# The lo half of stationary weights, 128 bytes further in SBUF

## The chip, the cores and the metric

The kernel runs on one core of a Trainium2 chip. The metric is the device time of one execution in microseconds (us), the median of several runs. Engines are called as in the profile: PE (TensorE matmuls), PEld (TensorE loading the stationary operand), DVE (VectorE), ACT (ScalarE), POOL (GpSimd), SP (the queue that issues DMAs).

## The reference, cut to what matters

Two layers of an encoder on 256 tokens of width 1024 in float32. Layer 0 is FFN, dilated attention, FFN; layer 1 is FFN, retention, FFN. Every sub-layer is normed before and after and added to the residual.

```
def swiglu(h, w_gate, w_up, w_down):
    return (jax.nn.silu(h @ w_gate) * (h @ w_up)) @ w_down
...
for i in range(DEPTH):                      # DEPTH = 2
    h = swiglu(rms_norm(x, g[0]), ...);  x = x + 0.5 * rms_norm(h, g[1])
    m = dilated_attention(...) if i % 2 == 0 else retention(...)
    x = x + rms_norm(m, g[3])
    h = swiglu(rms_norm(x, g[4]), ...);  x = x + 0.5 * rms_norm(h, g[5])
```

The widths: 1024 to 2816 for gate and for up, 2816 to 1024 for down (four such FFNs), 1024 to 9216 into attention, 1024 to 8192 into retention. Nearly all of the time goes to these products of 256 rows of input with a weight matrix that is read once from HBM.

## The kernel before, in words

**Three products for one.** Each float32 operand is cut into hi (rounded to the type float32r, which TensorE takes in one pass) and lo (what is left, also float32r). A product is then hi·hi + hi·lo + lo·hi, three matmuls into the same PSUM accumulator.

**The stream of weights.** `Stream` brings 128-row pieces of all weight matrices in the order in which they are used. A DMA of 1 MB on SP fills `raw` (two buffers); `split` then takes 1024 columns of it: ACT writes hi, scaled by the gain of the norm (line 121), DVE writes lo (line 122), in two halves of 512 columns. Both lie in one buffer `w` of a ring of six, each of 2112 floats per partition (`WC`, 64 floats more than the 2048 needed). A few pieces at the start of a sub-layer go to other buffers (`wx`, from `extra`), hi and lo at their start and middle. When PE has finished with a piece, `done` asks for the next split into that ring buffer.

**Two forms of matmul.** In `piece` and `down` (lines 192 to 194, helper `mm3`) 128 columns of the input are stationary, and 512 columns of the weight move. In `unit_t` (lines 381 to 383) it is the other way round: 128 columns of the weight are loaded as the stationary operand, and 256 columns of the input move. For each block of 128 weight columns there are three matmuls, which this document calls a triple:

```
mm(out, hi[:, s], xh, ...)   # line 381: load hi, move xh
mm(out, hi[:, s], xl, ...)   # line 382: load hi again, move xl
mm(out, lo[:, s], xh, ...)   # line 383: load lo, move xh
```

`unit_t` is used for all but the first gate and up block of each FFN, and for the queries and keys of the attention after its first unit. The pieces that it uses are marked in `Stream.still`.

**Where the operands lie.** Counted in bytes of one partition, modulo 256: the input tiles `xh` and `xl` lie at 0, with a row of 1280 bytes for each 128 channels, so that every moving operand begins at 0. The six ring buffers begin at 0 as well. In a piece that is in `still`, hi begins at 16 floats (64 bytes), and lo 1024 floats further, so at 64 again. The blocks of 128 columns are 512 bytes apart, so all loads of hi and of lo in `unit_t` begin at 64. In all other pieces hi and lo begin at 0.

The order of the work is the order in which the program is written; each engine takes its instructions in turn, and waits for others by semaphores.

Of the kernel before, what the change touches and what calls it, by code (L numbers as in the profile page):

```python
# [27 lines left out]
class Stream:  # L28
# [67 lines left out]
    def split(self):  # L96
        if self.n_split >= len(self.pieces):
            return
        i = self.n_split
        self.n_split += 1  # L100
        g, j, gain = self.pieces[i]
        while self.n_dma <= g:
            self.dma()
        nc = self.K.nc
        raw = self.raw[g][:, j * 1024 : (j + 1) * 1024]
        if i in self.extra:
            both = self.K.sb.tile([P, 2, 1024], F32R, tag=self.extra[i], name=f"wx{i}")
            hi, lo = both[:, 0], both[:, 1]
        else:

            both = self.K.sb.tile([P, WC], F32R, tag="w", bufs=self.ring, name=f"w{i}")
            o = 16 if i in self.still else 0
            hi, lo = (both[:, z : z + 1024] for z in (o, o + 1024))
        if gain is None:
            nc.scalar.activation(hi, raw, AF.Copy)  # L115
            nc.vector.tensor_tensor(out=lo, in0=raw, in1=hi.bitcast(F32), op=ALU.subtract)  # L116
        else:
            for kk in range(2):
                s = slice(kk * 512, kk * 512 + 512)
                gc = self.K.gcol[:, gain + kk : gain + kk + 1]  # L120
                nc.scalar.activation(hi[:, s], raw[:, s], AF.Copy, scale=gc)  # L121
                nc.vector.scalar_tensor_tensor(  # L122
                    out=lo[:, s], in0=raw[:, s], scalar=gc, in1=hi[:, s].bitcast(F32),
                    op0=ALU.mult, op1=ALU.subtract,
                )
        self.tiles[i] = (hi, lo)
        if j == 1:
            del self.raw[g]
            while self.n_dma < len(self.groups) and self.n_dma <= g + self.raw_bufs:
                self.dma()  # L130
# [927 lines left out]
```

## Time and profile before

| | |
|---|---|
| median of 3 runs (lowest to highest) | 1292.06 us (1289.16 to 1293.95) |
| the profiled execution, its own time | 1295.78 us |
| its span, first to last instruction | 1294.0 us |
| PE busy, PEld busy | 99%, 88% of the span |
| DVE, ACT, POOL busy | 69%, 54%, 2% |
| share of PE in the chain of work that ended last | 90% |
| granted TensorE clock | 0.998 |
| read from HBM | 232 MB, 180 GB/s over the span |

How to read it: matmuls are pipelined, each one's end is modelled, and the spans of matmuls that follow each other overlap. A busy PE is thus no measure of its pace. The pace is the distance from the start of a matmul to the start of the next, which the timeline gives. PEld overlaps with PE: while one matmul runs, the stationary operand of the next is loaded.

### The profile page before, as it was taken

How to read it: one execution, taken by the hardware profiler on the slowest of the kernel's cores; microseconds unless marked ns; L12 is line 12 of the kernel's file. 1: busy time of each engine (PE TensorE's matmuls, PEld its weight loads, DVE VectorE, ACT ScalarE, POOL GpSimd, SP SyncE). 2: the span in 40 equal slices, each digit the busy share in tenths (PEclk: the TensorE clock that was granted, in tenths of full speed). 3: DMA queues.
4: the chain of work that ended last, by engine and by line, in shares of the span. 5: the costliest groups of instructions: out<-in, count | busy, mean ns of one | idle time of the engine just before them, and what ended most of it. 6: DMA issues, size and time to landing. Idle time of an engine off the chain costs nothing.

```text
span 1294.0 us, 20715 instructions
## 1 busy us (share of the span) xinstructions
PE 1276.6 (99%) x8362; PEld 1136.7 (88%) x8362; DVE 889.4 (69%) x1593; ACT 695.5 (54%) x1073; POOL 19.7 (2%) x17
## 2 busy tenths in 40 slices
PE   8999999999999999999999999999999999999997
PEld 6999888987997879999889998877888888899986
DVE  6776557678567668866477665588887875767644
ACT  4655445467445557764456554455555545555442
POOL 1000001000000000000000000000000000000000
PEclk9999999999999999999999999999999999999999
DMA  7755566664764356665546565645564645565551
GB/s 217 229 186 193 189 217 192 200 200 146 201 198 153 130 162 221 196 196 179 192 163 209 187 195 194 197 147 175 155 184 144 186 165 195 168 200 176 190 195 65
DMA packets 130093, 235.72 MB, mean 182 GB/s; under 512 B 25404, under 2 KB 42284, under 8 KB 129997
## 3 DMA queue, kind: packets, MB, share of 16 engines
q1 hardware_dynamic: 129852, 234.14, 56.7%
q8 instruction: 65, 1.06, 0.3%
q14 instruction: 32, 0.25, 0.1%
q10 hardware_dynamic: 144, 0.26, 0.1%
HBM read 232.21 MB, written 1.12 MB: 180 GB/s over the span
## 4 chain that ended last, share of the span: by engine, by line
PE 90%; DVE 4%; ACT 2%; DMA 2%; issue 1%; SPq 0%; DVEq 0%; ACTq 0%
PE ac_f L381 10%; PE ac_f L382 10%; PE ac_f L383 10%; PE d_f L192 6%; PE d_f L193 6%; PE d_f L194 6%; PE rt L194 4%; PE rt L193 4%; PE rt L192 4%; PE at L382 3%; PE at L383 3%; PE at L381 3%; PE at L192 2%; PE at L194 2%; DMA raw<-in_ret_w_in_dram 2%; PE at L193 2%
## 5 line engine op out<-in xcount | busy, mean ns | idle before, releaser
L121 ACT ACTIVATE w<-raw,gcol 128x512 fp32r<-128x512 f32 x596 | 394.0, 715 | 309.0 <-PE ac_f L383 101.9
L122 DVE SCALAR_TENSOR_TENSOR w<-raw,gcol,w 128x512 fp32r<-128x512 f32 x596 | 418.1, 749 | 153.9 <-ACT w L121 150.6
L116 DVE TENSOR_TENSOR w<-raw,w 128x1024 fp32r<-128x1024 f32 x112 | 137.2, 1225 | 134.5 <-ACT w L115 134.2
L115 ACT ACTIVATE w<-raw 128x1024 fp32r<-128x1024 f32 x112 | 118.8, 1061 | 166.7 <-PE d_f L194 95.7
L192 PE MATMUL d_f<-w,hhf 128*128 128x512 f32 x352 | 137.2, 390 | 0.0
L193 PE MATMUL d_f<-w,hhf 128*128 128x512 f32 x352 | 137.0, 389 | 0.0
L194 PE MATMUL d_f<-w,hlf 128*128 128x512 f32 x352 | 137.0, 389 | 0.0
L382 PE MATMUL at<-xl_f,w 128*128 128x256 f32 x352 | 99.0, 281 | 0.0
L381 PE MATMUL at<-xh_f,w 128*128 128x256 f32 x352 | 99.0, 282 | 0.0
L383 PE MATMUL at<-xh_f,w 128*128 128x256 f32 x352 | 98.9, 281 | 0.0
L192 PE MATMUL rt<-w,xh_f 128*128 128x512 f32 x244 | 95.6, 392 | 0.2 <-ACT xh_f L238 0.2
L193 PE MATMUL rt<-w,xh_f 128*128 128x512 f32 x244 | 95.8, 392 | 0.0
L194 PE MATMUL rt<-w,xl_f 128*128 128x512 f32 x244 | 95.1, 390 | 0.0
L381 PE MATMUL ac_f<-xh_at,w 128*128 128x256 f32 x288 | 81.0, 281 | 0.0
L381 PE MATMUL ac_f<-xh_f,w 128*128 128x256 f32 x288 | 81.0, 281 | 0.0
L381 PE MATMUL ac_f<-xh_rt,w 128*128 128x256 f32 x288 | 81.0, 281 | 0.0
L383 PE MATMUL ac_f<-xh_f,w 128*128 128x256 f32 x288 | 80.9, 281 | 0.0
L383 PE MATMUL ac_f<-xh_rt,w 128*128 128x256 f32 x288 | 80.9, 281 | 0.0
L383 PE MATMUL ac_f<-xh_at,w 128*128 128x256 f32 x288 | 80.9, 281 | 0.0
L382 PE MATMUL ac_f<-xl_at,w 128*128 128x256 f32 x288 | 80.9, 281 | 0.0
L382 PE MATMUL ac_f<-xl_f,w 128*128 128x256 f32 x288 | 80.9, 281 | 0.0
L382 PE MATMUL ac_f<-xl_rt,w 128*128 128x256 f32 x288 | 80.9, 281 | 0.0
(346 smaller groups left out, 2835.8 us busy)
## 6 DMA issues: line engine op xcount, KB each, us to landing
raw<-in_ffn_w_down_dram SPq DMA_DIRECT2D x44, 1024.0 KB, 4.9
raw<-in_ffn_w_up_dram SPq DMA_DIRECT2D x40, 1024.0 KB, 5.0
raw<-in_ffn_w_gate_dram SPq DMA_DIRECT2D x39, 1024.0 KB, 5.0
raw<-in_attn_w_in_dram SPq DMA_DIRECT2D x36, 1024.0 KB, 5.1
raw<-in_ret_w_in_dram SPq DMA_DIRECT2D x24, 1024.0 KB, 5.6
raw<-in_ret_w_in_dram SPq DMA_DIRECT2D x16, 512.0 KB, 3.9
raw<-in_ret_w_out_dram SPq DMA_DIRECT2D x8, 1024.0 KB, 4.8
raw<-in_ffn_w_gate_dram SPq DMA_DIRECT2D x10, 512.0 KB, 4.0
```

Of the source, the lines that this page charges most:

```text
L115: nc.scalar.activation(hi, raw, AF.Copy)
L116: nc.vector.tensor_tensor(out=lo, in0=raw, in1=hi.bitcast(F32), op=ALU.subtract)
L121: nc.scalar.activation(hi[:, s], raw[:, s], AF.Copy, scale=gc)
L122: nc.vector.scalar_tensor_tensor(out=lo[:, s], in0=raw[:, s], scalar=gc, in1=hi[:, s].bitcast(F32), op0=ALU.mult, op1=ALU.subtract,)
L192: mm(out, xh, wh, start=start, stop=False)
L193: mm(out, xh, wl, start=False, stop=False)
L194: mm(out, xl, wh, start=False, stop=stop)
L381: mm(out, hi[:, s], xh, start=k == 0 and a == 0, stop=False, skip_group_check=True)
L382: mm(out, hi[:, s], xl, start=False, stop=False, skip_group_check=True)
L383: mm(out, lo[:, s], xh, start=False, stop=k == NK - 1, skip_group_check=True)
```

## The change

In a piece that `unit_t` uses, lo begins at float 1072 and not at 1040 of its buffer. Hi stays at float 16. Modulo 256 bytes, hi begins at 64 as before and lo at 192. Other pieces stay as they were. Each engine has the same instructions in the same order, and all buffers have the same addresses; 1504 loads of lo in `unit_t` read, and 376 DVE instructions of line 122 write, 128 bytes further. The file has one line less, so that line 381 before is line 380 after.

```diff
             both = self.K.sb.tile([P, WC], F32R, tag="w", bufs=self.ring, name=f"w{i}")
-            o = 16 if i in self.still else 0
-            hi, lo = (both[:, z : z + 1024] for z in (o, o + 1024))
+            hi, lo = (both[:, z : z + 1024] for z in ((16, 1072) if i in self.still else (0, 1024)))
```

## The prediction

> **What bounds the kernel now.** I read the page's busy times and the chain of waits first, then the groups of instructions, then the timeline, where the pace of the matmuls can be seen.
>
> ```profile
> span 1294.0 us, 20715 instructions
> PE 1276.6 (99%) x8362; PEld 1136.7 (88%) x8362; DVE 889.4 (69%) x1593; ACT 695.5 (54%) x1073; POOL 19.7 (2%) x17
> PEclk9999999999999999999999999999999999999999
> PE 90%; DVE 4%; ACT 2%; DMA 2%; issue 1%; SPq 0%; DVEq 0%; ACTq 0%
> ```
>
> PE is busy nearly throughout, at a full granted clock, and has 90% of the chain that ended last. The others follow it: among the waits, ACT's longest ones inside the program are for PE to give back a ring buffer.
>
> ```profile
> ACT w L121 <- PE ac_f L383: 101.9, 75, 4.3
> L381 PE MATMUL at<-xh_f,w 128*128 128x256 f32 x352 | 99.0, 282 | 0.0
> L381 PE MATMUL ac_f<-xh_at,w 128*128 128x256 f32 x288 | 81.0, 281 | 0.0
> ```
>
> The matmuls that the change touches stand at lines 381 to 383: three lines with 352 in the attention and 4 x 288 in the FFNs, 3 x (352 + 4 x 288) = 4512, of which a third loads lo. A matmul's own 281 ns are modelled and overlap with the next; the pace is the distance of the starts. In the order of the timeline, first and last of a stretch each, 24 matmuls apart in the first FFN, 27 in the second, and 9 of the form with 512 moving columns:
>
> ```profile
> 109.85 0.28 PE L381 MATMUL ac_f<-xh_in,w 128*128 128x256 f32 x1
> ...
> 112.57 0.28 PE L381 MATMUL ac_f<-xh_in,w 128*128 128x256 f32 x1
> 539.78 0.28 PE L381 MATMUL ac_f<-xh_at,w 128*128 128x256 f32 x1
> ...
> 542.96 0.28 PE L381 MATMUL ac_f<-xh_at,w 128*128 128x256 f32 x1
> 620.10 0.39 PE L193 MATMUL d_f<-w,hhf 128*128 128x512 f32 x1
> ...
> 622.14 0.39 PE L193 MATMUL d_f<-w,hhf 128*128 128x512 f32 x1
> ```
>
> 2.72 / 24 = 113.3 ns, 3.18 / 27 = 117.8 ns, and 2.04 / 9 = 226.7 ns. The same instructions, on the same buffers, go at two paces. The windows say how far each reaches: some 354 starts in 40 us at the quick pace, 340 at the slow one (a window also counts two or three that began before it).
>
> ```profile
> 100.00:140.00 40.00, 40.00 (x356) 40.00 (x354) 26.32 (x36) 21.39 (x31) 0.00 (x0) 1.00 0.59 195
> 340.00:380.00 40.00, 40.00 (x342) 40.00 (x341) 23.75 (x35) 18.73 (x28) 0.00 (x0) 1.00 0.66 204
> 520.00:560.00 40.00, 40.00 (x342) 40.00 (x341) 31.58 (x49) 29.15 (x46) 0.00 (x0) 1.00 0.62 205
> 740.00:780.00 40.00, 40.00 (x342) 40.00 (x342) 26.72 (x38) 22.08 (x33) 0.00 (x0) 1.00 0.59 189
> 1170.00:1210.00 40.00, 40.00 (x342) 40.00 (x341) 26.52 (x39) 23.34 (x38) 0.00 (x0) 1.00 0.59 192
> ```
>
> The clock is 1.00 in all five, so it isn't the clock. Nor is it the feeding: PE has no idle time, and the quick window moves its bytes at the same DMA share (0.59) as the slow ones. What differs shows in the loads:
>
> ```profile
> L382 PEld LDWEIGHTS ac_f<-xl_in,w x288: 187/188/192, 37.8 to 139.8; 128*128 128x128 f32 x144
> L383 PE MATMUL ac_f<-xh_in,w x288: 276/276/384, 38.0 to 140.0; 128*128 128x256 f32 x144
> L383 PEld LDWEIGHTS ac_f<-xh_at,w 128*128 128x128 f32 x288 | 55.2, 192 | 0.0
> L382 PEld LDWEIGHTS ac_f<-xl_f,w 128*128 128x128 f32 x288 | 54.1, 188 | 0.0
> L381 PEld LDWEIGHTS ac_f<-xh_f,w 128*128 128x128 f32 x288 | 55.2, 192 | 0.0
> ```
>
> At the slow pace one load of each triple takes 192 ns in place of 188, and it is the lo load in one FFN and the first hi load in another. At the quick pace all take 188 in the median. And a stretch changes its pace only where something interrupts it, as here eight transposes do:
>
> ```profile
> 41.81 0.28 PE L382 MATMUL ac_f<-xl_in,w 128*128 128x256 f32 x1
> ...
> 43.34 0.28 PE L383 MATMUL ac_f<-xh_in,w 128*128 128x256 f32 x1
> 43.46 1.04 PE L416 MATMUL htr<-ident,h_f 128*128 128x128 f32 x8
> ...
> 44.80 0.28 PE L382 MATMUL ac_f<-xl_in,w 128*128 128x256 f32 x1
> ...
> 45.94 0.28 PE L383 MATMUL ac_f<-xh_in,w 128*128 128x256 f32 x1
> ```
>
> 13 matmuls in 1.53 us before (117.7 ns), 10 in 1.14 us after (114). So the load of the next stationary operand and the moving read of the current matmul get in each other's way, by how they stand to each other in time, and a stretch holds the rhythm in which it began. About 810 of the 4512 run at 113.3 (the first FFN's 864, less the 48 ahead of those transposes and a few around other interruptions, with some in the attention), the other 3,700 at 117.8.
>
> **The change, part by part.** *Instructions.* None is added, removed or moved, and no DMA changes; this part costs nothing because there is nothing to hide.
>
> *The DVE writes of lo*, 376 of them, land at 192 rather than 64 modulo 256. A write of lo at 0 (`wx`) against the mean of the ring's, of which most are at 64:
>
> ```profile
> L122 DVE SCALAR_TENSOR_TENSOR w<-raw,gcol,w 128x512 fp32r<-128x512 f32 x596 | 418.1, 749 | 153.9 <-ACT w L121 150.6
> L122 DVE SCALAR_TENSOR_TENSOR wx<-raw,gcol,wx 128x512 fp32r<-128x512 f32 x28 | 19.4, 748 | 8.2 <-ACT wx L121 8.2
> ```
>
> 1 ns apart, so 376 x 1 ns = 0.4 us either way, and DVE has 13 us free in each 40 of the windows. If it were longer, PE's own pace would still hide it. I take 0.
>
> *The loads of lo*, 1504 of them, are the whole question: their place against the moving read turns by half of 256 bytes, that of the hi loads stays. No row shows a load of the 256-column form at any place but 64, so I bound it. The good end is the quick pace throughout: 3,700 x (117.8 - 113.3 = 4.44 ns) = 16.4 us less. I take that pace as a floor of the moving side, since the form with 512 columns, where the loads have slack, goes at just twice 113.3. The bad end starts from the difference of the two paces in one triple, 3 x 4.44 = 13.3 ns: if the lo load collides where it did not, a triple loses half of that to all of it beyond the slow pace, 1504 x 6.7 = 10.0 us to 1504 x 13.3 = 20.0 us, and the 810 lose what they had, 810 x 4.44 = 3.6 us. I take the good end, because of the two paces seen it is the only one in which no load is prolonged, and because the slow one is a rhythm over three loads that stand alike: with one of the three turned by half a period, the rhythm that now repeats itself cannot stay as it is. That is a weak reason, and the chances say so.
>
> One rule speaks against any effect. The Trainium skill, page "SBUF — State Buffer", section "Who interferes with whom", gives PE two independent read ports, one for the moving operand and one for loads, and says that PE never waits on anyone. By it the place of lo would make 0 us; the two paces above disagree with it in this trace, by 4.44 ns a matmul. Another page, "TensorE: Matmul & The Clock Gate", section "Back-to-back issue gap", gives N / 2.4 + 2.5 ns, so an estimated 109.2 ns for 256 columns; by it the floor would be lower and 35 us could go (3,700 x 8.6 + 810 x 4.1 ns), which no row here shows.
>
> The sum: 1295.78 us of the profiled execution less 16.4 = 1279.4 us. That execution is 3.7 us above the median of the runs, 1292.06; against the median it makes 1275.7, and I forecast **1276 us**. What is saved on PE reaches the end, since ACT and DVE wait for PE and fed it without a gap at the quick pace.
>
> **The rivals.** *No change:* 1292 us. The paces may come from time alone, not from addresses: a stretch of equal addresses shows both, and half of 256 bytes may be a whole number of whatever steps the two reads share. Then each stretch locks as it did. Against it: a load that is prolonged at one alignment in time and not at another is what a conflict over banks of the memory would look like. This case also holds the outcome that all 4512 go at the slow pace: 3.6 us more, 1295.7.
>
> *Slower:* the lo load, turned, meets the moving read in every triple. Place: line 383's load in all stretches. Price: 10.0 + 3.6 us as above, 1305.7; at the far end 20.0 + 3.6, 1315.7. It decides from 6.5 us on, 4.3 ns per triple if the quick stretches stay quick. For it: nothing keeps a triple from taking a worse rhythm than the one seen, and two unlike neighbours may collide at times when equal ones don't. Against it: no stretch of this trace shows a pace worse than 117.8.
>
> *Half:* some stretches, or one load in the triple, get quick: a triple saves 6.7 ns, 3,700 / 3 x 6.7 = 8.3 us, 1283.8.
>
> **How the numbers follow.** Runs of this kernel spread over 0.37%, so 0.5% (6.5 us) is about what can be told from no change. The quick pace throughout: 0.33. Half: 0.11. No change, with the small loss: 0.28. Slower: 0.25 at 1299 to 1307 and 0.03 beyond. So faster 0.44, same 0.28, slower 0.28. The range must take in the good end, with 2.5 us for the median's own spread, 1273, and reach into the slower case up to its near price, 1306; some 0.15 are left out, most of it above. The forecast's own range is 1273 to 1284.
>
> **What would show it.** Right: in the windows some 356 matmuls in 40 us in every FFN and in the attention; triples of 340 ns in the timeline; no group of loads of these three lines (380 to 382 after the change) with a mean of 192; groups of the 512-column form unchanged at 390 ns with starts 226.7 apart; DVE's line 122 at 749. The no-change rival shows 342 per window with the same stretches quick and slow. The slower one shows fewer than 342, with the lo group's loads above 188 in all FFNs. What would make me wrong: the reads conflict by some other period than 256 bytes, or a stretch's rhythm is set by how it begins whatever the addresses are.

## The result, and the profile after

| | before | after |
|---|---|---|
| median (lowest to highest) of 4 runs | 1292.64 us (1289.16 to 1293.95) | 1281.24 us (1280.75 to 1281.66) |
| ratio, 95% interval | | 0.9909 (0.9883 to 0.9934) |
| the profiled execution, its span | 1295.78, 1294.0 us | 1281.66, 1279.9 us |

The change makes the kernel 0.9% faster. (The four runs of after include the profiled one; the profiled one of before is not among its four.) The head of the page of after reads as that of before: PE is still busy 99% of the span, with 91% of the chain. The busy share does not show what happened, since the pace changed and not the idle time.

```profile
span 1279.9 us, 20715 instructions
PE 1261.3 (99%) x8362; PEld 1120.3 (88%) x8362; DVE 886.1 (69%) x1593; ACT 695.3 (54%) x1073; POOL 19.3 (2%) x17
PE 91%; DVE 4%; ACT 2%; DMA 2%; issue 1%; SPq 0%; DVEq 0%; ACTq 0%
```

The windows of after show it: 340 to 380 us lies in the attention, 520 to 560 in the second FFN, 1170 to 1210 in the last one. (PE's busy time is followed by its count of matmuls.)

```profile
340.00:380.00 40.00, 40.00 (x356) 40.00 (x355) 24.33 (x36) 20.08 (x30) 0.00 (x0) 1.00 0.70 211
520.00:560.00 40.00, 40.00 (x356) 40.00 (x354) 31.57 (x49) 28.52 (x44) 0.00 (x0) 1.00 0.65 210
1170.00:1210.00 40.00, 40.00 (x355) 40.00 (x355) 25.93 (x36) 22.36 (x34) 0.00 (x0) 1.00 0.56 185
```

Where before had 342 matmuls in 40 us, after has 355 or 356, at the same clock of 1.00. Counted over all starts in the trace, 1457 of the 1476 triples that nothing interrupts take 340 ns (within 3 ns, most within 1); before it was 264, and 1211 took 353 to 355 ns. The modelled length of a matmul follows its pace, 281 ns at the slow one and 276 at the quick one, so that the view of a source line shows the same at a glance. The line of the first hi load, two groups before and the same two after (shortest, median, longest ns, then the first and the last start in us):

```profile
L381 PE MATMUL ac_f<-xh_in,w x288: 276/276/388, 37.8 to 139.8; 128*128 128x256 f32 x144
...
L381 PE MATMUL ac_f<-xh_rt,w x288: 281/281/363, 1123.4 to 1225.7; 128*128 128x256 f32 x144
```

```profile
L380 PE MATMUL ac_f<-xh_in,w x288: 276/276/388, 39.4 to 141.2; 128*128 128x256 f32 x144
...
L380 PE MATMUL ac_f<-xh_rt,w x288: 276/276/364, 1113.1 to 1211.6; 128*128 128x256 f32 x144
```

The 288 of this line in the last FFN took 102.3 us before and 98.5 after. The same rows show that after began its first FFN 1.6 us later than this execution of before did.

How a stretch finds its pace can be read in the timeline. Both kernels are interrupted in the attention and begin again at a slow pace. In the kernel after:

```profile
328.93 0.28 PE L381 MATMUL at<-xl_f,w 128*128 128x256 f32 x1
...
330.24 0.28 PE L380 MATMUL at<-xh_f,w 128*128 128x256 f32 x1
...
330.58 0.28 PE L380 MATMUL at<-xh_f,w 128*128 128x256 f32 x1
330.69 0.28 PE L381 MATMUL at<-xl_f,w 128*128 128x256 f32 x1
330.81 0.28 PE L382 MATMUL at<-xh_f,w 128*128 128x256 f32 x1
330.92 0.28 PE L380 MATMUL at<-xh_f,w 128*128 128x256 f32 x1
```

The first 11 matmuls take 1.31 us, 119.1 ns each. From 330.24 on a triple takes 340 ns, and it stays so for the remaining 179 triples of the stretch. In before, the stretch that began at the same place stayed at 117.8 ns to its end: the slow rhythm lasts there, and does not last after the change.

DVE's line that writes lo takes 748 ns in the mean (749 before), and the 512-column form 226.7 ns from start to start, as before.

### The profile page after: what moved, and what is told of

It is laid out like the page before. It is cut to its first block, busy times and chain, and to the rows that moved or that the text cites. A ratio compares the mean times of both kernels' runs of the same rounds, so it can differ in the third digit from the quotient of the medians.

```text
span 1279.9 us, 20715 instructions
## 1 busy us (share of the span) xinstructions
PE 1261.3 (99%) x8362; PEld 1120.3 (88%) x8362; DVE 886.1 (69%) x1593; ACT 695.3 (54%) x1073; POOL 19.3 (2%) x17
## 4 chain that ended last, share of the span: by engine, by line
PE 91%; DVE 4%; ACT 2%; DMA 2%; issue 1%; SPq 0%; DVEq 0%; ACTq 0%
PE ac_f L382 10%; PE ac_f L380 10%; PE ac_f L381 10%; PE d_f L193 6%; PE d_f L191 6%; PE d_f L192 6%; PE rt L193 4%; PE rt L192 4%; PE rt L191 4%; PE at L380 3%; PE at L382 3%; PE at L381 3%; PE at L191 2%; PE at L193 2%; PE at L192 2%; PE ac_f L192 2%
## 5 line engine op out<-in xcount | busy, mean ns | idle before, releaser
L380 PE MATMUL at<-xh_f,w 128*128 128x256 f32 x352 | 97.4, 277 | 0.0
L382 PE MATMUL at<-xh_f,w 128*128 128x256 f32 x352 | 97.3, 276 | 0.0
L380 PE MATMUL ac_f<-xh_in,w 128*128 128x256 f32 x288 | 79.9, 278 | 0.0
L382 PE MATMUL ac_f<-xh_in,w 128*128 128x256 f32 x288 | 79.7, 277 | 0.0
L380 PE MATMUL ac_f<-xh_rt,w 128*128 128x256 f32 x288 | 79.6, 276 | 0.0
L380 PE MATMUL ac_f<-xh_at,w 128*128 128x256 f32 x288 | 79.6, 276 | 0.0
L380 PE MATMUL ac_f<-xh_f,w 128*128 128x256 f32 x288 | 79.6, 276 | 0.0
L381 PE MATMUL ac_f<-xl_in,w 128*128 128x256 f32 x288 | 79.5, 276 | 0.0
L382 PE MATMUL ac_f<-xh_at,w 128*128 128x256 f32 x288 | 79.5, 276 | 0.0
L382 PE MATMUL ac_f<-xh_rt,w 128*128 128x256 f32 x288 | 79.5, 276 | 0.0
L382 PE MATMUL ac_f<-xh_f,w 128*128 128x256 f32 x288 | 79.5, 276 | 0.0
```

The lines of the kernel that those rows point to most:

```text
L380: mm(out, hi[:, s], xh, start=k == 0 and a == 0, stop=False, skip_group_check=True)
L381: mm(out, hi[:, s], xl, start=False, stop=False, skip_group_check=True)
L382: mm(out, lo[:, s], xh, start=False, stop=k == NK - 1, skip_group_check=True)
```

## The experiments

Each of the runs below but the last was executed once, under the profiler; what is compared is the pace in its trace. Of single times, differences below some 7 us are not told apart where a kernel has both paces, since the runs of before alone reach from 1288.91 to 1296.25. The runs below came from two chips; the same program, before, shows its triples of 340 and 353 to 354 ns on both. Places are bytes modulo 256.

**Both halves at 192.**

```diff
-... ((16, 1072) if i in self.still else (0, 1024)))
+... ((48, 1072) if i in self.still else (0, 1024)))
```

> Hi and lo both begin at 192 modulo 256 (before: both at 64; after: 64 and 192). Theory 1, the rhythm: a quick stretch needs hi and lo half a turn (128 bytes) apart, so with both alike most stretches stay at 117.8 ns a matmul, and the time is about 1292 us (1289 to 1296). Theory 2, the place: 192 is a good place for a load beside a moving read at 0 and 64 is a poor one, so with both at 192 all stretches go at 113.3 ns or better, and the time is 1281 us or less.

1300.82 us, 117.8 ns in 1473 of 1476 triples. The first FFN too, quick in before and after:

```profile
95.00:135.00 40.00, 40.00 (x342) 40.00 (x341) 25.98 (x38) 22.02 (x34) 0.00 (x0) 1.00 0.57 185
```

So 192 is not a good place by itself; theory 2 falls. And in this run no load is prolonged, though all matmuls go at the slow pace. The loads of hi, of hi again and of lo in the second FFN:

```profile
L380 PEld LDWEIGHTS ac_f<-xh_at,w 128*128 128x128 f32 x288 | 54.1, 188 | 0.0
L381 PEld LDWEIGHTS ac_f<-xl_at,w 128*128 128x128 f32 x288 | 54.1, 188 | 0.0
L382 PEld LDWEIGHTS ac_f<-xh_at,w 128*128 128x128 f32 x288 | 53.9, 187 | 0.0
```

The load of 192 ns that went with the slow pace in before is thus not what makes a pace slow.

**Hi at 0 and lo at 128; hi at 64 and lo at 128; hi at 32 and lo at 160.**

```diff
-... ((16, 1072) if i in self.still else (0, 1024)))
+... ((0, 1056) if i in self.still else (0, 1024)))     # hi0_lo128
+... ((16, 1056) if i in self.still else (0, 1024)))    # hi64_lo128
+... ((8, 1064) if i in self.still else (0, 1024)))     # hi32_lo160
```

> Hi at 0 and lo at 128: half a turn apart as in the kernel after, but both 64 bytes lower, hi where the moving operand begins. Theory 1 (half a turn between the two is what matters): 113.3 ns in all stretches, about 1281 us. Theory 2 (192 is the good place): no load is at 192, so the slow pace or worse, 1290 us or more.

> Hi at 64 as in both kernels, lo at 128: a quarter turn apart. Theory 1, strict form (half a turn is needed): some stretches slow, a triple between 340 and 353 ns, 1284 to 1293 us. Theory 1, loose form (any difference breaks the rhythm over three loads): 340 ns in all triples, 1281 us. Theory 2: lo isn't at 192, so slow, about 1292 us.

> Hi at 32 and lo at 160: half a turn apart, each 32 bytes below the kernel after. If steps of 64 bytes are what the two reads share, this is neither the after (64, 192) nor the slow (0, 128): a pace between 113.3 and 119.1 ns, 1281 to 1306 us. Theory 3 in its loose form (any place off the moving read's, half a turn apart): 113.3 ns, 1281 us.

1306.03, 1302.64 and 1302.94 us. The mean pace of all uninterrupted matmuls is 119.1, 118.2 and 118.4 ns, and no triple in any of the three takes 340 ns. A window from the second FFN for each, in the same order:

```profile
520.00:560.00 40.00, 40.00 (x338) 40.00 (x338) 32.71 (x58) 31.02 (x48) 0.00 (x0) 1.00 0.61 197
```

```profile
520.00:560.00 40.00, 40.00 (x340) 40.00 (x340) 33.01 (x55) 31.04 (x48) 0.00 (x0) 1.00 0.62 202
```

```profile
520.00:560.00 40.00, 40.00 (x340) 40.00 (x339) 32.98 (x55) 30.88 (x49) 0.00 (x0) 1.00 0.60 196
```

With 338 to 340 matmuls all are slower in these windows than the slow pace of before (342). Half a turn between hi and lo is in two of them, and does not help; theory 1 falls in both its forms. Theory 3's loose form, any place off the moving read's with half a turn between, falls with the last.

**Hi and lo exchanged.**

```diff
-... ((16, 1072) if i in self.still else (0, 1024)))
+... ((1072, 16) if i in self.still else (0, 1024)))
```

> Hi at 192 and lo at 64: the kernel after with the two places exchanged. Half a turn alone did not make the quick pace (hi at 0 and lo at 128: slower than before), nor did 192 for both (117.8 ns throughout). Theory 3, both together: the two places off the moving read's, 64 and 192, taken by unlike neighbours. It expects 113.3 ns a matmul in all stretches, about 1281 us. Theory 4, the order: only the lo load, which runs beside the moving xl, may be at 192; then two of three loads at 192 behave as three did, 117.8 ns, about 1300 us.

1297.14 us, and neither: 509 triples take 340 ns, nearly all of the other 967 take 352 to 361, in stretches that keep what they have. The attention, and the second and third FFN:

```profile
340.00:380.00 40.00, 40.00 (x339) 40.00 (x338) 24.88 (x37) 18.77 (x28) 0.00 (x0) 1.00 0.64 205
520.00:560.00 40.00, 40.00 (x355) 40.00 (x355) 32.65 (x51) 31.20 (x49) 0.00 (x0) 1.00 0.62 199
710.00:750.00 40.00, 40.00 (x339) 40.00 (x338) 24.96 (x37) 21.92 (x35) 0.00 (x0) 1.00 0.57 185
```

The same two places, taken the other way round, have two lasting rhythms, of which the slow one is slower than that of before. So it counts which loads of the triple stand where, one of three at 192 (64, 64, 192) or two (192, 192, 64). Theory 3 asked for quick stretches throughout, theory 4 for none.

**The input's lo tile moved instead.** Hi and lo stay at 64; the moving operand of line 382 begins at 128.

```diff
-        self.xl = self.sb.tile([P, NK, XC], F32R, tag="xl", name=f"xl_{name}")
+        xl = self.sb.tile([P, NK * XC + 64], F32R, tag="xl", name=f"xl_{name}")
+        self.xl = xl[:, 32 : 32 + NK * XC].rearrange("p (k c) -> p k c", c=XC)
```

> Hi and lo both at 64 as in the kernel before; the input's lo tile xl lies 128 bytes further instead, so that the moving operand of line 382 begins at 128. The load of lo runs beside that matmul, so it stands to the moving read next to it as in the kernel after (64 - 128 = 192 modulo 256), and the loads of hi as before. Theory 5, only the place of a load relative to the moving read beside it counts: 113.3 ns in all stretches, about 1281 us. Theory 6, what counts is the row of loads itself (64, 64, 192), whatever moves: no change, mostly 117.8 ns, 1292 to 1296 us. In matmuls of the other form, 496 loads of xl now begin at 128; where they don't matter those stay at 226.7 ns.

1304.49 us; 117.8 ns in the mean, and no triple at 340. A window in the second FFN:

```profile
520.00:560.00 40.00, 40.00 (x342) 40.00 (x341) 33.09 (x55) 31.02 (x49) 0.00 (x0) 1.00 0.60 197
```

The place of each load relative to the read beside it was that of the kernel after, and the quick pace did not come: theory 5 falls, as far as a load meets one read only. (The record of a load is 188 ns long and matmuls start 113 ns apart, so a load may meet the next read too.) Theory 6 is not shown by it either, since the quick stretches of the first FFN went too, so the moving row (0, 128, 0) has an effect of its own. The 512-column form, a part of whose loads now begin at 128, went from 227.3 to 229.1 ns in the mean of its uninterrupted starts.

**The other pieces at 64 and 192 too.**

```diff
-... ((16, 1072) if i in self.still else (0, 1024)))
+... (16, 1072))
```

> The kernel after, with hi at 64 and lo at 192 in the ring's other pieces too, whose columns move in the 512-column form (the loads there, xh and xl, stay at 0). If 226.7 ns is the floor of the moving read (twice 113.3), the 512-column form stays there and the time is 1281 us. If it is a collision with the loads as the 117.8 ns are, some 2,700 matmuls can go to 222 ns or less and save 10 us or more, or lose as much where the new places are worse.

1290.16 us. The matmuls of the change stay quick (1448 triples at 340 ns); the 512-column form loses, 230.2 ns in the mean against 227.3. From the down product of the second FFN, 20 matmuls:

```profile
639.83 0.40 PE L191 MATMUL d_f<-w,hhf 128*128 128x512 f32 x1
...
644.44 0.39 PE L193 MATMUL d_f<-w,hlf 128*128 128x512 f32 x1
```

4.61 us / 20 = 230.5 ns. Over 2,769 uninterrupted starts 2.9 ns make 8.0 us, and the time is 8.9 us above the median of after.

**Half the load.** In before and in after, seven eighths of the loads are halved.

```diff
+                    if k:
+                        out, s = out[:64], slice(s.start, s.start + 64)
                     mm(out, hi[:, s], xh, ...)
```

> The kernel before, but from the second block of 128 channels on (k > 0, seven eighths of the matmuls of this form) only 64 of the 128 weight columns are loaded as the stationary operand; the moving read stays as it is. The other 64 columns of those products are left out. If the slow pace is the load of 128 columns hindered by the moving read, and the load is what the next matmul waits for, half a load leaves slack and the slow pace goes: 113.3 ns (340 ns a triple) or less, about 1281 us or less. If the pace is set on the moving side whatever the load, the slow pace stays at 117.8 ns, 1292 to 1296 us.

> The same halving of loads in the kernel after (the other 64 columns are left out from the second block of channels on). If 113.3 ns is a floor of the moving read, it stays at 113.3 ns and 1281 us. If 113.3 ns too is a load that comes late, it goes below: at 109 ns some 3,900 matmuls save 17 us, about 1264 us.

1298.58 us for before and 1281.11 for after. The loads are shorter, here in the lo group of the attention, of before:

```profile
L384 PEld LDWEIGHTS at<-xh_f,w 128*64 128x64 f32 (+1 forms) x352 | 49.7, 141 | 0.0
```

The mean of 141 ns mixes 308 halved loads with 44 full ones of 188; a halved load alone takes 134 ns ((352 x 141 - 44 x 188) / 308). The attention and the last FFN, of before with half loads and then of after with half loads:

```profile
340.00:380.00 40.00, 40.00 (x339) 40.00 (x338) 24.96 (x37) 18.73 (x28) 0.00 (x0) 1.00 0.67 206
1150.00:1190.00 40.00, 40.00 (x355) 40.00 (x354) 27.82 (x42) 24.24 (x38) 0.00 (x0) 1.00 0.60 189
```

```profile
340.00:380.00 40.00, 40.00 (x355) 40.00 (x354) 24.77 (x37) 19.87 (x30) 0.00 (x0) 1.00 0.70 214
1150.00:1190.00 40.00, 40.00 (x355) 40.00 (x354) 27.73 (x42) 22.40 (x36) 0.00 (x0) 1.00 0.62 199
```

Before still has slow stretches (and, this time, a quick last FFN), and after stays at 113.3 ns. The slow pace did not stay as it was: the slow triples of before take 118.9 ns a matmul in the mean with halved loads, 117.8 with full ones. A load that takes some 53 ns less does not bring the next matmul sooner at either pace. So the matmul does not wait for the end of a load that comes late. That the place of the load changes the pace of the moving side instead is argued from this, not shown.

**Before, twice more, and after once more,** word for word.

> The kernel before, word for word, profiled once more. If the pace of a stretch is set by the moment at which it begins, other stretches than in the first profile are quick this time, and the execution's time goes with the number of matmuls at the slow pace by 4.44 ns each: 1295.8 us had some 3,700. If the pace belongs to the place in the program, the same stretches are quick (the first FFN) and the time is again 1294 to 1297 us.

> The kernel before once more. If a stretch takes its rhythm from the moment at which it begins, the quick stretches are again some of the first FFN and by chance others; two profiles had about 810 and 1,220 quick matmuls. If the rhythm belongs to the place in the program, the same as in the first profile.

> The kernel after once more, timed. If its quick rhythm is the only one that lasts, every stretch again ends at 113.3 ns whatever its beginning, the runs differ by less than those of before, and the time is 1280 to 1283 us, 0.9 to 1.2% below before. If the first profile was a lucky one, some stretches stay at 117.8 ns, 1283 to 1293 us.

| kernel | profiled execution, us | triples at 340 ns | triples at 353 to 355 ns |
|---|---|---|---|
| before, first profile | 1295.78 | 264 | 1211 |
| before again, 1 | 1295.75 | 400 | 1074 |
| before again, 2 | 1292.40 | 624 | 849 |
| after, first profile | 1281.66 | 1457 | 0 |
| after again | 1281.39 | 1462 | 1 |

The third FFN of before, in its second and in its third profile:

```profile
710.00:750.00 40.00, 40.00 (x342) 40.00 (x341) 25.27 (x37) 22.29 (x36) 0.00 (x0) 1.00 0.58 185
```

```profile
710.00:750.00 40.00, 40.00 (x355) 40.00 (x354) 26.43 (x40) 22.40 (x36) 0.00 (x0) 1.00 0.62 199
```

One program, one place in it, and both paces: which one a stretch of before gets differs from execution to execution. (These two profiles are from two chips. On the chip of the third, seven runs of before reach from 1288.91 to 1295.55 us, so the chip alone does not settle the time.) After, timed against before in three rounds, took 1281.36 us (1279.27 to 1281.43) against 1293.76 (1288.91 to 1295.55), ratio 0.9902 (0.9874 to 0.993). Its stretches all ended quick in both profiles. Of its eight executions, all but one (1279.27) lie within 1 us of each other.

No kernel tried that computes the whole product was faster than the one after.

## Why the prediction was right or wrong

**Two paces, and the good end.** Right, and the time lies in the forecast's own range. The forecast was that all stretches reach 113.3 ns, and 1457 of 1476 triples do. The starts of the matmuls of this form, summed where nothing interrupts, went from 524.1 to 508.1 us: 16.0 us, where the prediction had 16.4.

**The sum against the median.** This term was mis-sized: 11.4 us between the medians, for 16.4. From one profiled execution to the other it is 14.1; the 1.6 us by which after began its first FFN later make up most of what lacks there. The rest is the step from the execution to the median. The prediction took the 3,700 slow matmuls of the execution at 1295.78 us and subtracted them all from the median of 1292.06. But the executions of before differ in these matmuls and in when their first FFN begins. The third profile had 849 slow triples and not 1211, 362 x 13.3 = 4.8 us less, began that FFN 1.2 us later, and took 3.4 us less. The second had 137 fewer, 1.8 us, began it 1.5 us later, and took the same time. An execution at the median need not hold all the slow matmuls of the slowest one. How many the unprofiled ones held is not measured.

**"A stretch holds the rhythm in which it began."** Right for before, and a likely reason for its spread of 0.5% against 0.2% or less after; the paces of the unprofiled runs are not known. After, a stretch does not hold a slow beginning: 119.1 ns in the rows above, then 113.3. With halved loads, two stretches of before turned from slow to quick without an interruption as well, after 20 and 16 triples.

**The floor.** The step that took 113.3 ns as the moving side's floor agrees with all runs: half the load did not lower it, nor did any of the nine placements that were profiled; the 512-column form never went below twice as much. The Trainium skill, "TensorE: Matmul & The Clock Gate", section "Back-to-back issue gap", gives N / 2.4 + 2.5 ns, an estimated 109.2 ns for 256 columns, for a single matmul by itself and not for a stream with loads, to which the prediction applied it. This case's traces measure 113.3 at best, with half loads too. What sets the 113.3 stays open.

**The reason for taking the good end** failed, so the outcome, which had been given a chance of 0.33, was right by luck. The prediction argued that a rhythm over three equal loads cannot stay when one of them is turned by half a period. Half a turn at other places (0 and 128, 32 and 160) made the mean pace slower than in before, 119.1 and 118.4 ns. And the step "the load of the next stationary operand and the moving read get in each other's way" was taken as a load that comes late; the half loads show that the matmul doesn't wait for it. The other reason, that only at the quick pace no load is prolonged, fails with both halves at 192: 117.8 ns, and no group of those loads above 188.

**No change, and its rule.** The Trainium skill, "SBUF — State Buffer", section "Who interferes with whom", has PE wait on no one. This case's traces disagree: of the placements alone, with the same instructions, the mean pace goes from 113.4 to 119.1 ns.

**Slower.** It did not happen to this change, but it did with hi at 0 and lo at 128: 1306.03 us, where the near price was 1305.7. The case was real, and nothing in the trace of before told the two apart. That the numbers meet is in part luck: the price put 13.6 us on the median, by 6.7 ns a triple beyond the slow pace, while these matmuls took 9.5 us more than in the first profile of before (533.6 for 524.1), 4.0 ns a triple beyond the slow pace.

**DVE.** Right in the time of line 122: 748 ns. The free time was read too high for one window: at 520 us DVE was busy for 31.58 of 40, so it had 8.4 us free there and not 13. Its writes moved together with the loads, and no run parts the two. But of the 1451 triples of after that take 340 ns within 1, 995 overlap in time with a write of lo and 456 with none, so the quick pace does not hang on the writes.

What remains open is why 64, 64, 192 leaves only the quick rhythm. That it is the place modulo 256 is supported by the ring, whose buffers differ by multiples of 256 bytes and share one pace, and by the difference between (64, 64), (192, 192) and (64, 192), which would be one and the same modulo 128. Which reads share what is not shown.

## What to carry to other kernels

Where matmuls with a load each follow without a gap, take the pace from start to start, stretch by stretch: two paces of one instruction on the same buffers, at the same clock, went here with a place of the operands that mattered, and no busy share showed it. Try places of the stationary operand one at a time, on the chip and with the order in which they are loaded, since neighbouring choices here made between 0.9% less and about 1% more time, and no rule for them came out. A kernel whose runs spread may hold such a mixture of paces: profile it more than once before you subtract one execution's stalls from the median of others.

## What the runs showed of the hardware that was not expected

- The same stretch of the same program (the third FFN of before) ran at 113.3 or 117.8 ns a matmul in different executions, and kept its pace for up to 815 matmuls.
- Placements of the stationary operand alone moved the mean pace of the 256-column form from 113.4 ns (64, 192) over 117.8 (192, 192) to 119.1 (0, 128).
- Loads of 64 columns in place of 128 (134 ns in place of 188) left the quick pace at 113.3 ns, and made the slow one of before slower, 118.9 for 117.8.
- A load of 192 ns in place of 188 goes with the slow pace at (64, 64) and not at (192, 192), at 117.8 ns both times.
- Moving reads at 64 and 192 in place of 0 slowed the 512-column form from 227.3 to 230.2 ns in the mean.
